# Attention with one score product: probabilities turned on TensorE, and two heads' values on two column halves

## The chip, the core and the metric

The kernel runs on one core of a Trainium2 chip. TensorE (PE) multiplies matrices from SBUF into PSUM; VectorE (DVE), ScalarE (ACT) and GpSimd (POOL) work on rows of both memories; SyncE (SP) and the queues of ACT and POOL issue DMAs. The metric is the device time of one execution in microseconds. The profile is one execution's own record: its *span* goes from the first to the last instruction.

## The reference

One layer of a hybrid encoder takes 1024 tokens of a new stream and 32 tokens of a running one (1056 in all, width 1024). One input projection feeds three mixers: latent attention, an S5 state-space model and an RWKV-7 scan. Their outputs (384, 256 and 384 wide) go through one output projection, a layer norm, and an MLP of squared ReLU. The change is in attention, of 6 heads:

```python
def mla_scores(q_nope, q_rope, k_nope, k_rope):
    s = jnp.einsum('bqhd,bkhd->bhqk', q_nope, k_nope) + jnp.einsum('bqhr,bkr->bhqk', q_rope, k_rope)
    return s.astype(F32) * MLA_SCALE

def attend(s, v, mask=None):
    if mask is not None:
        s = jnp.where(mask, s, NEG_INF)
    p = jax.nn.softmax(s, axis=-1).astype(v.dtype)
    return jnp.einsum('bhqk,bkhd->bqhd', p, v)
```

A head's key has 64 columns of its own and 32 rotary ones shared by the heads; values have 64. Prompt tokens see the 64-token chunks up to their own (the mask); sample tokens see all of 512 cached keys and the 32 new ones.

## The kernel before, in words

The program goes through the input projection, the matrices of the scan, a *middle* part, the output projection with its norm, and the MLP. The middle (from about 246 to 692 us) runs four streams, each a Python generator that yields after a short step: F (`attn_front`), O (`attn_back`), S (the RWKV scan, nine blocks of 128 tokens, the sample's first) and X (S5). `PLAN` is a string with one letter a step. `middle` takes the next letter, makes that stream's step, and lays the step behind the last PE instruction of the step before, so PE's order follows the string closely; two rules turn an F into an O and back when one of them is too far ahead. Within these bounds a scheduler sets the order on the other engines.

Every matrix product that needs near-f32 accuracy and is long is done by `mm3`: each operand is split into a high and a low part of type f32r (`split3`, an ACT copy and a DVE subtraction), and three matmuls (lines 63, 65 and 67) add up. Other products are f32 matmuls, which the profile records as two passes.

Before, a head makes its scores twice. In F, `attn_max` puts tokens on partitions (tile `sc`, one PSUM bank of two, up to 512 keys), masks, and takes each token's maximum on DVE (line 1227). The maxima of nine token tiles are turned on PE (`scm`), split, and sent by four small DMAs into row 96 of the head's query tiles `qh`, `ql`, where the keys hold -1. In O, `attn_out` then puts keys on partitions (tile `st`, up to 512 tokens, 97 rows at work): the maximum is subtracted by the product itself, ACT takes the exponential to `ptk` (line 1281), POOL zeroes the masked quarter (line 1283), and the result is already the moving operand of the value product `av` (line 1256), up to 512 tokens wide. The stationary operand is 128 wide: 64 value columns and 64 columns of ones, so that the sum of the probabilities comes out on the other 64 partitions. Lines 1261 to 1269 copy `av` out (`po`), and multiply by the reciprocal of the sum, made from Ln, Exp and one Newton step, to `ot`. Token blocks are 512, the 32 sample tokens, and 512. Heads 2p and 2p+1 make pair p, which fills 128 rows of `mg_d` in DRAM.

Keys are kept for three heads (`NKT`), queries for two. The queries of all heads are written to DRAM (`q_d`) by `stage_q` and read back by `attn_q`. Behind the middle, `out_early` loads the mixers' outputs of three token tiles into the room of keys and queries, and `out_mm` begins the output projection (`acc<-wo,mh`); the scheduler lays these matmuls among the last attention steps.

In the scan each step uses PE and then DVE or ACT; its PE tiles are named `pra`, `prt`, `prb`, `prk`, `prg`, `pru`, `prn`, `pry`, `prs`, `prm`, `prw`, `prv`, from a ring of three PSUM banks. Most of its matmuls use 64*64 tiles of the array.

Of the kernel before, what the change touches and what calls it, by code (L numbers as in the profile page):

```python
# [8 lines left out]
F32 = mybir.dt.float32  # L9
# [1079 lines left out]
def attn_setup(g):  # L1089

    nc = g.nc
    g.kh, g.kl, g.q2 = [], [], []
# [8 lines left out]
    for x in (kr, g.kpast):  # L1101
        nc.gpsimd.memset(x[96:128], 0.0)
        nc.gpsimd.memset(x[96:97], -1.0)
    for x, o, c, n in ((g.kpast, TP, 0, 512), (kr, 0, 0, TP), (kr, 1536, TP, TS)):
        split3(g, x[64:128, c:c + n], g.kh[0][64:128, o:o + n], g.kl[0][64:128, o:o + n])
    for i in range(NKT):
        for ks in (g.kh, g.kl):
            if i:
                nc.gpsimd.tensor_copy(out=ks[i][64:128], in_=ks[0][64:128])
        for x in g.q2[i] if i < 2 else ():  # L1110
            nc.scalar.activation(out=x[96:128], in_=g.ckv[96:128], func=AF.Copy, scale=0.0)
# [15 lines left out]
def attn_values(g, p):  # L1127

    nc = g.nc
    vo = g.ap.tile([P, 13, 3, 64], F32, tag="vo", name="vo", bufs=1)  # L1130
    nc.gpsimd.memset(vo[:, :, 1], 1.0)
    for q in range(0, 13, 4):
# [6 lines left out]
        nc.scalar.activation(out=vo[:n, q:q + m, 0:3:2], in_=ps[:n, :m].rearrange("p t (h x) -> p t h x", h=2), func=AF.Copy)  # L1139
# [57 lines left out]

def attn_q(g, h):

    nc = g.nc  # L1200
    qh, ql = g.q2[h % 2]
    q = g.ap.tile([P, T], F32, tag="q", name="q", bufs=1)
    nc.sync.dma_start(out=q[0:96], in_=g.q_d[h])
    if h > 1:
        for x in (qh, ql):
            nc.scalar.activation(out=x[96:128], in_=g.kh[0][96:128, 0:T].bitcast(F32), func=AF.Copy, scale=0.0)
# [3 lines left out]
    return qh, ql  # L1210


def attn_max(g, h, qh, ql):

    nc = g.nc
    kh, kl = g.kh[h % NKT], g.kl[h % NKT]
    mx = g.ap.tile([P, 9, 2], F32, tag="mx", name="mx", bufs=2)
    nc.gpsimd.memset(mx, -3.0e38)
    for t in range(9):
        s, n, k0, nk = (t * P, P, 0, (t + 1) * P) if t < 8 else (TP, TS, 1024, 544)  # L1220
        for b in range(0, nk, 512):
            w = min(512, nk - b)
            ps = g.psc.tile([P, 512], F32, tag="sc", name="sc")
            mm3(nc, [ps[:n, :w]], qh[:, s:s + n], ql[:, s:s + n], [(kh[:, k0 + b:k0 + b + w], kl[:, k0 + b:k0 + b + w])], True, True)
            if t < 8 and b + w == nk:
                nc.vector.memset(ps[0:64, w - 64:w], -1e30)
            nc.vector.tensor_reduce(out=mx[:n, t, b // 512:b // 512 + 1], in_=ps[:n, :w], axis=AX.X, op=ALU.max)  # L1227
            yield
    yield
    yield  # L1230
    m9 = g.ap.tile([P, 9], F32, tag="m9", name="m9", bufs=2)
    nc.vector.tensor_tensor(out=m9, in0=mx[:, :, 0], in1=mx[:, :, 1], op=ALU.max)
    ps = g.psc.tile([P, 512], F32, tag="sc", name="scm")
    nc.tensor.transpose(out=ps[0:9, 0:P], in_=m9, identity=g.ident)
    mh = g.ap.tile([9, P], F32R, tag="mh", name="mh", bufs=2)
    ml = g.ap.tile([9, P], F32R, tag="ml", name="ml", bufs=2)
    split3(g, ps[0:9, 0:P], mh, ml)
    for m, q in ((mh, qh), (ml, ql)):
        nc.sync.dma_start(out=q[96:97, 0:TP].bitcast(F32), in_=m[0:8].bitcast(F32))
        nc.sync.dma_start(out=q[96:97, TP:T].bitcast(F32), in_=m[8:9, 0:TS].bitcast(F32))  # L1240


def attn_out(g, h, qh, ql, vo, ot):

    nc = g.nc
    i = h % 2
    kh, kl = g.kh[h % NKT], g.kl[h % NKT]
    rows, srow = hsl(i), hsl(1 - i)
    late = None

    def av(s, n, kt, c, w, pt, tiles, po=[None]):

        if kt == tiles[0]:
            po[0] = g.pav.tile([P, 512], F32, tag="av", name="av")
        po = po[0]
        nc.tensor.matmul(out=po[:, c:n], lhsT=vo[:w, kt].rearrange("p a x -> p (a x)")[:, 64 * i:64 * i + P], rhs=pt[:w, c:n],  # L1256
                         start=kt == tiles[0], stop=kt == tiles[-1])
        if kt < tiles[-1]:
            return
        x = g.ap.tile([P, 512], F32, tag="ptk", name="po", bufs=g.npt)  # L1260
        nc.scalar.activation(out=x[:, :n], in_=po[:, :n], func=AF.Copy)  # L1261
        rec = g.ap.tile([P, 512], F32, tag="rec", name="rec", bufs=1)
        rt = g.ap.tile([P, 512], F32, tag="rt", name="rt", bufs=1)
        nc.scalar.activation(out=rec[srow, :n], in_=x[srow, :n], func=AF.Ln)
        nc.scalar.activation(out=rec[rows, :n], in_=rec[srow, :n], func=AF.Exp, scale=-1.0)
        nc.vector.tensor_copy(out=rt[rows, :n], in_=x[srow, :n])
        nc.vector.tensor_tensor(out=rt[rows, :n], in0=rt[rows, :n], in1=rec[rows, :n], op=ALU.mult)
        nc.vector.scalar_tensor_tensor(out=rec[rows, :n], in0=rt[rows, :n], scalar=2.0, in1=rec[rows, :n], op0=ALU.subtract, op1=ALU.mult)
        nc.vector.scalar_tensor_tensor(out=ot[rows, s:s + n], in0=x[rows, :n], scalar=-1.0, in1=rec[rows, :n], op0=ALU.mult, op1=ALU.mult)
        if i == 1:  # L1270
            store(g, nc.sync if h == 5 and s == 512 else None, g.mg_d[h // 2, :, s:s + n], ot[:, s:s + n])

    for s, n in ((0, 512), (TP, TS), (512, 512)):
        tiles = range((s + n) // P) if n > TS else range(8, 13)
        for kt in tiles:
            c = max(0, kt * P - s) if n > TS else 0
            w = P if kt < 12 else TS
            ps = g.pst.tile([P, 512], F32, tag="st", name="st")
            mm3(nc, [ps[:w, c:n]], kh[:, kt * P:kt * P + w], kl[:, kt * P:kt * P + w], [(qh[:, s + c:s + n], ql[:, s + c:s + n])], True, True)
            pt = g.ap.tile([P, 512], F32, tag="ptk", name="ptk", bufs=g.npt)  # L1280
            nc.scalar.activation(out=pt[:w, c:n], in_=ps[:w, c:n], func=AF.Exp, scale=MLA_SCALE)
            if n > TS and kt * P >= s:
                nc.gpsimd.memset(pt[64:128, c:c + 64], 0.0)
# [4 lines left out]
            late = s, n, kt, c, w, pt, tiles  # L1288
    av(*late)


NKT = 3
# [7 lines left out]
def attn_front(g):  # L1300
# [4 lines left out]
    for h in range(6):  # L1305
        if h % 2 == 0:
            yield from attn_keys(g, h // 2)
# [1088 lines left out]
```

## Time and profile before

| what | value |
|---|---|
| median of 3 runs (lowest, highest) | 1469.61 us (1469.31, 1478.45) |
| profiled execution | 1466.29 us |
| its span | 1464.5 us |
| granted PE clock, mean | 0.976 |

In a row of a stretch stands the busy time of each engine, with its number of instructions. In a row of the timeline stand start and duration of one or several equal instructions; on PE the durations of neighbours overlap. "128*64" is the part of the array that a matmul uses, rows by columns, and "128x512" what one instruction works on. A wait is put down to whatever released the waiting instruction last.

### The profile page before, as it was taken

What the parts mean: (1) busy time and instruction counts of PE and PEld (TensorE: products, weight loads), DVE (VectorE), ACT (ScalarE), POOL (GpSimd) and SP (SyncE); (2) the same over time, 40 slices, a digit from 0 to 9 for tenths busy, and PEclk for the clock granted to TensorE, in tenths of its full rate; (3) what the DMA queues carried; (4) which work ended last, traced back from release to release, by engine and by line L of the source; (5) the groups of instructions that cost most, each with busy time, mean ns of one, the idle gap of its engine ahead of it and who ended that gap; (6) DMA issues with size and microseconds to landing.
All of it is one profiled execution on the core that took longest, in us unless ns stands there. A gap on an engine that the chain in (4) does not pass through costs nothing.

```text
span 1464.5 us, 28210 instructions
## 1 busy us (share of the span) xinstructions
PE 1376.6 (94%) x11527; PEld 1237.8 (85%) x11527; DVE 986.2 (67%) x1752; ACT 643.6 (44%) x1126; POOL 186.5 (13%) x285
## 2 busy tenths in 40 slices
PE   7999999698999879889899899999999999999996
PEld 6989898476777657667589899999999999999995
DVE  8767979654656635653858976666656686665577
ACT  5544645334554554542426444444444443334332
POOL 2412110401111111220530000000000000000023
PEclk9999999899999989989999999999999999999998
DMA  5315464671343320241634344443329795354222
GB/s 201 146 67 189 143 183 101 150 154 50 91 106 87 87 54 28 70 122 44 201 119 138 129 182 136 162 143 145 142 89 386 256 307 176 91 178 131 62 102 76
DMA packets 150326, 198.59 MB, mean 136 GB/s; under 512 B 53392, under 2 KB 98116, under 8 KB 149688
## 3 DMA queue, kind: packets, MB, share of 16 engines
q1 hardware_dynamic: 129396, 175.91, 37.4%
q10 hardware_dynamic: 20448, 19.88, 4.4%
q8 instruction: 90, 1.47, 0.4%
q0 software_dynamic: 352, 1.01, 0.2%
q14 instruction: 40, 0.33, 0.1%
HBM read 129.42 MB, written 67.28 MB: 134 GB/s over the span
## 4 chain that ended last, share of the span: by engine, by line
PE 79%; DVE 8%; DMA 5%; ACT 3%; issue 2%; SPq 1%; ACTq 0%; POOL 0%; DVEq 0%; POOLq 0%
PE acc L63 20%; PE acc L65 20%; PE acc L67 19%; PE av L1256 3%; PE st L65 1%; PE st L63 1%; PE st L67 1%; DVE mx L1227 1%; PE prw L883 1%; PE sc L63 1%; PE scv L1138 1%; DMA xr<-in_xt 1%; DMA mraw<-mg_d 1%; PE prt L841 1%; DMA wr<-in_w_up 1%
## 5 line engine op out<-in xcount | busy, mean ns | idle before, releaser
L63 PE MATMUL acc<-xo,wo 128*128 128x272 f32 (+1 forms) x896 | 254.8, 285 | 2.8 <-ACT wo L49 2.8
L67 PE MATMUL acc<-xo,wo 128*128 128x256 f32 (+1 forms) x896 | 253.9, 285 | 1.9 <-DVE wo L50 1.9
L65 PE MATMUL acc<-xo,wo 128*128 128x272 f32 (+1 forms) x896 | 253.7, 284 | 0.0
L67 PE MATMUL acc<-hop,wo 128*128 128x272 f32 (+1 forms) x896 | 193.9, 283 | 0.0
L63 PEld LDWEIGHTS acc<-xo,wo 128*128 128x128 f32 x896 | 168.8, 189 | 3.0 <-ACT wo L49 3.0
L67 PEld LDWEIGHTS acc<-xo,wo 128*128 128x128 f32 x896 | 168.8, 189 | 2.3 <-DVE wo L50 2.3
L65 PEld LDWEIGHTS acc<-xo,wo 128*128 128x128 f32 x896 | 169.1, 189 | 0.0
L65 PE MATMUL acc<-hop,wo 128*128 128x272 f32 (+1 forms) x768 | 158.6, 284 | 0.0
L63 PE MATMUL acc<-hop,wo 128*128 128x256 f32 (+1 forms) x768 | 158.3, 284 | 0.0
L67 PEld LDWEIGHTS acc<-hop,wo 128*128 128x128 f32 x896 | 142.7, 188 | 0.0
L63 PE MATMUL acc<-xh,wmhi 128*128 128x384 f32 (+3 forms) x384 | 127.6, 333 | 7.8 <-ACT xh L49 7.8
L65 PE MATMUL acc<-xl,wmhi 128*128 128x384 f32 (+3 forms) x384 | 128.3, 334 | 2.5 <-DVE xl L50 2.5
L67 PE MATMUL acc<-xh,wmlo 128*128 128x384 f32 (+3 forms) x384 | 126.1, 328 | 0.0
L65 PEld LDWEIGHTS acc<-hop,wo 128*128 128x128 f32 x768 | 119.2, 188 | 0.0
L63 PEld LDWEIGHTS acc<-hop,wo 128*128 128x128 f32 x768 | 118.1, 188 | 0.0
L2134 POOL TENSOR_TENSOR wr<-wr,gb 128x512 f32<-128x512 f32 (+1 forms) x14 | 19.8, 1437 | 672.6 <-ACT wr L2132 672.6
L49 ACT ACTIVATE wo<-wr 128x512 fp32r<-128x512 f32 (+1 forms) x64 | 47.0, 739 | 117.1 <-PE acc L67 70.1
L1256 PE MATMUL av<-ptk,vo 128*128 128x512 f32 (+5 forms) x204 | 74.9, 453 | 14.0 <-ACT po L1261 9.3
L63 PEld LDWEIGHTS acc<-xh,wmhi 128*128 128x128 f32 (+1 forms) x384 | 71.3, 186 | 10.6 <-ACT xh L49 8.3
L50 DVE TENSOR_TENSOR hop<-hraw,hop 128x1056 fp32r<-128x1056 f32 (+3 forms) x58 | 70.4, 1213 | 14.3 <-ACT hop L49 14.2
L50 DVE TENSOR_TENSOR wo<-wr,wo 128x512 fp32r<-128x512 f32 (+1 forms) x64 | 52.3, 820 | 39.4 <-ACT wo L49 39.4
L65 PEld LDWEIGHTS acc<-xl,wmhi 128*128 128x128 f32 (+1 forms) x384 | 71.4, 186 | 7.2 <-DVE xl L50 3.9
(543 smaller groups left out, 3086.6 us busy)
## 6 DMA issues: line engine op xcount, KB each, us to landing
hraw<-h_d SPq DMA_DIRECT2D x48, 528.0 KB, 3.6
wr<-in_w_up SPq DMA_DIRECT2D x35, 512.0 KB, 3.9
h_d<-hx SPq DMA_DIRECT2D x16, 792.0 KB, 3.3
h_d<-ht SPq DMA_DIRECT2D x16, 792.0 KB, 4.6
wd<-in_w_dn SPq DMA_DIRECT2D x16, 512.0 KB, 6.2
wr<-in_w_dn SPq DMA_DIRECT2D x16, 512.0 KB, 5.0
ld<-rw SPq DMA_DIRECT2D x24, 320.0 KB, 4.5
wmraw<-in_w_m SPq DMA_DIRECT2D x12, 512.0 KB, 4.5
```

The source lines that it names most:

```text
L49: nc.scalar.activation(out=hi, in_=ps, func=AF.Copy)
L50: (lo_eng or nc.vector).tensor_tensor(out=lo, in0=ps, in1=hi.bitcast(F32), op=ALU.subtract)
L63: nc.tensor.matmul(out=outs[i], lhsT=lh, rhs=rhs[i][0], start=start, stop=False, **kw)
L65: nc.tensor.matmul(out=outs[i], lhsT=lh, rhs=rhs[i][1], start=False, stop=False, **kw)
L67: nc.tensor.matmul(out=outs[i], lhsT=ll, rhs=rhs[i][0], start=False, stop=stop, **kw)
L841: nc.tensor.transpose(out=pt[:, i], in_=ld[:, p, i], identity=g.ident)
L883: nc.tensor.matmul(out=pw[hsl(c), p - p0, h], lhsT=g.xt[p][hsl(c), t, h], rhs=r[hsl(c), p, K_A:K_NV + 1:K_NV, h], start=True, stop=True)
L1138: nc.tensor.matmul(out=ps[:n, j], lhsT=c, rhs=g.wkv[:, 1, p * P:p * P + P], start=True, stop=True)
L1227: nc.vector.tensor_reduce(out=mx[:n, t, b // 512:b // 512 + 1], in_=ps[:n, :w], axis=AX.X, op=ALU.max)
L1256: nc.tensor.matmul(out=po[:, c:n], lhsT=vo[:w, kt].rearrange("p a x -> p (a x)")[:, 64 * i:64 * i + P], rhs=pt[:w, c:n], start=kt == tiles ...
L2134: nc.gpsimd.tensor_tensor(out=o[:n, c], in0=o[:n, c], in1=g.gb2[:n, 0, c], op=ALU.mult)
```

## The change

Scores are made once, with tokens on partitions, and the exponential is taken there. `attn_rows` (stream F) goes through groups of one token tile, for both heads of a pair: product and masked maximum per part of up to 512 keys as before, then the smaller of the two negated maxima times the scale (DVE), then the exponential straight from the score banks with that as bias, which also adds up the row (`accum_out`). A score bank is so held until its exponential is done. The probabilities of a group and head stay in SBUF (`p`, six buffers).

`attn_out` (stream O) then turns each key tile's probabilities on PE, for two heads into one bank (`pt`), copies them out by DVE or ACT in turn (`ptk`, two buffers), and multiplies: each head has 64 value columns as stationary operand, on its own column half of the array, so that the two heads' outputs fill the 128 partitions of one bank. Masked keys are already zero, as the exponential of a masked score. The reciprocal of each token's sum is made on a column of 128 tokens, spread over 64 columns (`nb`), and turned on PE into the same bank (columns from 256 on); one DVE operation multiplies at the end. Ones in the values, POOL's zeroes, row 96 and its DMAs go. The shared key rows are copied between the two key buffers by two DMAs of ACT's queue and no longer by POOL. The query loads are issued one head ahead.

`PLAN` is another string, 557 letters and not 527; S and X have as many as before (132, 38).

```diff
-    kr = g.ap.tile([P, 13 * 3 * 64], F32, tag="vo", name="kr", bufs=1)[:, :T]
+    kr = g.ap.tile([P, T], F32, tag="q", name="kr", bufs=NQB)
...
-                nc.gpsimd.tensor_copy(out=ks[i][64:128], in_=ks[0][64:128])
+            nc.scalar.dma_start(out=ks[i][64:96].bitcast(F32), in_=ks[0][64:96].bitcast(F32))
...
+GROUPS = ((0,), (1,), (2,), (3,), (8,), (4,), (5,), (6,), (7,))
+def attn_rows(g, p, j):
+    sm = g.ap.tile([P, 2, 2, 2], F32, tag="sm", name="sm", bufs=2)
+    for i in range(2):
+        (qh, ql), kt = g.q2[i], (2 * p + i) % NKT
+        kh, kl = g.kh[kt], g.kl[kt]
+        for r, t in enumerate(GROUPS[j]):
+            s, n, k0, nk = (t * P, P, 0, (t + 1) * P) if t < 8 else (TP, TS, 1024, 544)
+            x = g.ap.tile([P, 1024], F32, tag="p", name="p", bufs=NPB)
...
+            for c, b in enumerate(range(0, nk, 512)):
+                if c:
+                    yield
+                w = min(512, nk - b)
+                ps = g.psc.tile([P, 512], F32, tag="sc", name="sc")
+                mm3(nc, [ps[:n, :w]], qh[0:96, s:s + n], ql[0:96, s:s + n], [(kh[0:96, k0 + b:k0 + b + w], kl[0:96, k0 + b:k0 + b + w])], True, True)
+                if t < 8 and b + w == nk:
+                    nc.vector.memset(ps[0:64, w - 64:w], -1e30)
+                nc.vector.tensor_reduce(out=mx[:n, c:c + 1], in_=ps[:n, :w], axis=AX.X, op=ALU.max, negate=True)
+                parts.append((ps[:n, :w], b, w))
...
+            for c, (ps, b, w) in enumerate(parts):
+                nc.scalar.activation(out=x[:n, b:b + w], in_=ps, func=AF.Exp, scale=MLA_SCALE, bias=mx[:n, 2:3], accum_out=sm[:n, i, r, c:c + 1])
+            xs[i, r] = x
+            yield
...
+def attn_out(g, p, j, vo, ot):
...
+    S.activation(out=y, in_=a, func=AF.Ln)
+    S.activation(out=y, in_=y, func=AF.Exp, scale=-1.0)
+    V.tensor_tensor(out=t, in0=a, in1=y, op=ALU.mult)
...
+        V.scalar_tensor_tensor(out=nb[:n, r], in0=bc(t[:, :, r:r + 1], [n, 2, 64]), scalar=2.0, in1=bc(y[:, :, r:r + 1], [n, 2, 64]), op0=ALU.subtract, op1=ALU.mult)
+    po = g.pav.tile([P, 512], F32, tag="av", name="av")
+    for r in range(m):
+        nc.tensor.matmul(out=po[:, 256 + n * r:256 + n * r + n], lhsT=nb[:n, r].rearrange("p i x -> p (i x)"), rhs=g.ident[:n, :n], start=True, stop=True)
+    S.activation(out=rb, in_=po[:, 256:256 + n * m], func=AF.Copy)
+    def av(k, w, c, halves, first, last):
+        for i in range(2):
+            nc.tensor.matmul(out=po[hsl(i), c:n * m], lhsT=vo[:w, k, 64 * i:64 * i + 64], rhs=halves[i], start=first, stop=last, tile_position=(0, 64 * i))
...
+        for k in range(last + 1):
...
+                    nc.tensor.transpose(out=ps[:, i, (r - r0) * P:(r - r0) * P + P], in_=xs[i, r][:, k * P:k * P + P], identity=g.ident)
...
+            if k % 2:
+                S.activation(out=e, in_=ps, func=AF.Copy)
+            else:
+                V.tensor_copy(out=e, in_=ps)
+            yield
+            if late:
+                av(*late)
+                yield
+            late = k, P, r0 * P, [e[:, i] for i in range(2)], k == 0, k == last
+        av(*late)
+    V.scalar_tensor_tensor(out=ot[:, s:s + n * m], in0=po[:, 0:n * m], scalar=-1.0, in1=rb, op0=ALU.mult, op1=ALU.mult)
...
-NKT = 3
+NKT = 2
+NPB = 6
+NPT = 2
+NQB = 1
...
-            if c == "F" and fronts > backs + 1:
+            if c == "F" and g.probs >= NPB:
                 c = "O"
...
-    "FFFFFFFFFFFSFFFFFFSFFFFFFSFFFFSFFFFSOOOSOFSOOOSFOOSOOOOSFSSOSFOOOOFSOOSXFOOOSFOOSXOOOOFFOOOSFSSSOSSO"
+    "FFFFFFFFSFFFFFFFFSFSOSFFSFSFOSOSSOOSOFSOFSOFOSOOSOFSOSXXFOSOFOSFOSFOSOFSOFSOFOSXOFSOFSOSFOXSSOSFOFOF"
```

What this moves on PE shows at two places. First, in the scan's stretch, between the state products (`pry`, `prs`) of a block and its `prw`. Before:

```order
L941 MATMUL pry<-gq,st 64x64 x6
L945 MATMUL prs<-st,gq 64x64 x6
L63 MATMUL sc<-kh,qh 128x256
L65 MATMUL sc<-kl,qh 128x256
L67 MATMUL sc<-kh,ql 128x256
L969 MATMUL prm<-yb,bones 128x384
L883 MATMUL prw<-r,xt 64x128 x12
L1256 MATMUL av<-ptk,vo 128x512
L63 MATMUL st<-qh,kh 128x512
L65 MATMUL st<-ql,kh 128x512
L67 MATMUL st<-qh,kl 128x512
```

Now, at the same place of a block:

```order
L1275 MATMUL av<-ptk,vo 64x128 x2
L941 MATMUL pry<-gq,st 64x64 x6
L945 MATMUL prs<-st,gq 64x64 x6
L1300 MATMUL pt<-ident,p 128x128 x2
L63 MATMUL sc<-kh,qh 128x512
L65 MATMUL sc<-kl,qh 128x512
L67 MATMUL sc<-kh,ql 128x512
L969 MATMUL prm<-yb,bones 128x384
L883 MATMUL prw<-r,xt 64x128 x12
```

The second score product (`st`) and the wide `av` are gone; a pair of turns (`pt`) or of 64-column `av` stands beside a scan step, and one score triple between F steps as before.

Second, behind the scan's last matmul (`prv`). Before:

```order
L986 MATMUL prv<-sq,bones 128x384
L1256 MATMUL av<-ptk,vo 128x512
L63 MATMUL st<-qh,kh 128x512
L65 MATMUL st<-ql,kh 128x512
L67 MATMUL st<-qh,kl 128x512
```

Now, some rows behind `prv`:

```order
L1130 MATMUL scv<-wkv,ckv 128x128 x4
L1130 MATMUL scv<-wkv,cpast 128x128 x4
L1130 MATMUL scv<-wkv,ckv 32x128
L1269 MATMUL av<-ident,nb 128x128
L1300 MATMUL pt<-ident,p 128x128 x2
L1275 MATMUL av<-ptk,vo 64x128 x2
L63 MATMUL sc<-kh,qh 128x512
L65 MATMUL sc<-kl,qh 128x512
L67 MATMUL sc<-kh,ql 128x512
```

Before, only the last head's second half stood there; now pair 2 begins there, with its values (`scv`) and its first token tiles, and the rest of its scores, turns and value products follow behind the scan's end, with no scan step among them.

More of the change, by code (lines that the diff above doesn't have):

```diff
@@ L1099, in attn_setup @@
             g.q2.append([g.ap.tile([P, T], F32R, tag=f"q{x}{i}", name="q" + x, bufs=1) for x in "hl"])
-    for x in (kr, g.kpast):
-        nc.gpsimd.memset(x[96:128], 0.0)
-        nc.gpsimd.memset(x[96:97], -1.0)
     for x, o, c, n in ((g.kpast, TP, 0, 512), (kr, 0, 0, TP), (kr, 1536, TP, TS)):
-        split3(g, x[64:128, c:c + n], g.kh[0][64:128, o:o + n], g.kl[0][64:128, o:o + n])
-    for i in range(NKT):
+        split3(g, x[64:96, c:c + n], g.kh[0][64:96, o:o + n], g.kl[0][64:96, o:o + n])
+    for i in range(1, NKT):
         for ks in (g.kh, g.kl):
-            if i:
-                nc.gpsimd.tensor_copy(out=ks[i][64:128], in_=ks[0][64:128])
-        for x in g.q2[i] if i < 2 else ():
-            nc.scalar.activation(out=x[96:128], in_=g.ckv[96:128], func=AF.Copy, scale=0.0)
+            nc.scalar.dma_start(out=ks[i][64:96].bitcast(F32), in_=ks[0][64:96].bitcast(F32))
 def attn_keys(g, p):
@@ L1129, in attn_values @@
     nc = g.nc
[L1130 to L1131 removed]
+    vo = g.ap.tile([P, 13, P], F32, tag="vo", name="vo", bufs=1)
     for q in range(0, 13, 4):
@@ L1138, in attn_values @@
             nc.tensor.matmul(out=ps[:n, j], lhsT=c, rhs=g.wkv[:, 1, p * P:p * P + P], start=True, stop=True)
-        nc.scalar.activation(out=vo[:n, q:q + m, 0:3:2], in_=ps[:n, :m].rearrange("p t (h x) -> p t h x", h=2), func=AF.Copy)
+        n = P if q < 12 else TS
+        nc.scalar.activation(out=vo[:n, q:q + m], in_=ps[:n, :m], func=AF.Copy)
         yield
@@ L1195, in stage_q, with attn_load @@
         nc.gpsimd.dma_start(out=g.q_d[4 + h, 64:96], in_=qb[32 * h:32 * h + 32])
+def attn_load(g, h):
+    g.qr[h] = g.ap.tile([P, T], F32, tag="q", name="q", bufs=NQB)
+    g.nc.sync.dma_start(out=g.qr[h][0:96], in_=g.q_d[h])
 def attn_q(g, h):
-    nc = g.nc
     qh, ql = g.q2[h % 2]
[L1202 to L1206, printed above, removed]
+    q = g.qr.pop(h)
     for s, n in ((0, 512), (512, 544)):
@@ L1209, in attn_q @@
         yield
-    return qh, ql
-def attn_max(g, h, qh, ql):
+GROUPS = ((0,), (1,), (2,), (3,), (8,), (4,), (5,), (6,), (7,))
+GM = max(map(len, GROUPS))
+def attn_rows(g, p, j):
     nc = g.nc
[L1216 to L1227, printed above, removed]
-            yield
[L1229 to L1240, printed above, removed]
@@ L1243, in attn_out @@
-def attn_out(g, h, qh, ql, vo, ot):
-    nc = g.nc
[L1246 to L1283, printed above, removed]
@@ L1287, in attn_out @@
                 yield
-            late = s, n, kt, c, w, pt, tiles
-    av(*late)
-NKT = 3
+            late = k, P, r0 * P, [e[:, i] for i in range(2)], k == 0, k == last
+        av(*late)
+    V.scalar_tensor_tensor(out=ot[:, s:s + n * m], in0=po[:, 0:n * m], scalar=-1.0, in1=rb, op0=ALU.mult, op1=ALU.mult)
+    g.probs -= 2 * m
+    store(g, nc.sync if p == 2 and j == len(GROUPS) - 1 else None, g.mg_d[p, :, s:s + n * m], ot[:, s:s + n * m])
+NKT = 2
+NPB = 6
+NPT = 2
+NQB = 1
 def last_traced(g, engine):
@@ L1304, in attn_front @@
     attn_setup(g)
-    for h in range(6):
-        if h % 2 == 0:
-            yield from attn_keys(g, h // 2)
-        g.qs[h] = yield from attn_q(g, h)
-        yield from attn_max(g, h, *g.qs[h])
-        yield h
-def attn_back(g):
-    for h in range(6):
-        if h % 2 == 0:
-            g.vo = yield from attn_values(g, h // 2)
-            g.ot = g.ap.tile([P, T], F32, tag="ot", name="ot", bufs=1)
-        yield from attn_out(g, h, *g.qs.pop(h), g.vo, g.ot)
-        yield h
+    g.qr = {}
+    for h in range(NQB):
+        attn_load(g, h)
+    for p in range(3):
+        yield from attn_keys(g, p)
+        for i in range(2):
+            h = 2 * p + i
+            yield from attn_q(g, h)
+            if h + NQB < 6:
+                attn_load(g, h + NQB)
+        for j in range(len(GROUPS)):
+            yield from attn_rows(g, p, j)
+            yield j
+def attn_back(g):
+    for p in range(3):
+        vo = yield from attn_values(g, p)
+        ot = g.ap.tile([P, T], F32, tag="ot", name="ot", bufs=1)
+        for j in range(len(GROUPS)):
+            yield from attn_out(g, p, j, vo, ot)
+            yield j
 def middle(g, scan):
-    g.npt, g.qs, g.late = 5, {}, []
+    g.late, g.probs = [], 0
     streams = {"F": attn_front(g), "O": attn_back(g), "S": scan, "X": stage_s5(g)}
```

59 lines of the change are left out of this document (52 added, 7 removed).

## The prediction

> **What bounds the kernel now.** I read the page's head first, then the busy time by stretches, the waits of TensorE (PE) in the attention stretch, and last the times at which single PE instructions start. The columns of the stretches are PE, its weight loads, DVE, ACT and POOL busy, the granted clock, the DMA share and the rate.
>
> ```profile
> PE 1376.6 (94%) x11527; PEld 1237.8 (85%) x11527; DVE 986.2 (67%) x1752; ACT 643.6 (44%) x1126; POOL 186.5 (13%) x285
> ```
>
> ```profile
> 246.00:308.00 62.00, 48.12 (x510) 34.72 (x510) 42.41 (x76) 23.44 (x47) 18.12 (x20) 0.86 0.66 151
> 308.00:667.00 359.00, 321.67 (x3488) 242.08 (x3482) 204.49 (x447) 180.80 (x373) 55.47 (x115) 0.95 0.30 81
> 667.00:689.00 22.00, 22.00 (x92) 16.37 (x91) 3.09 (x7) 4.22 (x10) 3.42 (x7) 1.00 0.05 14
> ```
>
> The program is held by PE nearly throughout. Only 246 to 689 us is touched: in the middle row attention (streams F and O), the RWKV scan (S) and S5 (X) share PE, which is busy 90% of it, DVE 57%, ACT 50%. So PE work taken out counts there, unless waits take its place. The waits that PE has in 246 to 692 (total, times, longest):
>
> ```profile
> PE sc L63 <- DVE mx L1227: 11.7, 11, 2.9
> ...
> PE av L1256 <- ACT po L1261: 9.3, 2, 8.7
> PE av L1256 <- POOL ptk L1283: 4.7, 5, 2.4
> PE st L63 <- DMA qh<-mh: 2.4, 1, 2.4
> ...
> PE st L65 <- DMA ql<-ml: 1.5, 2, 1.0
> ```
>
> **PE work removed.** A matmul's own duration holds pipeline time that overlaps the next, so I price by distances of starts. How many there are:
>
> ```profile
> L63 PE MATMUL st<-qh,kh x102: 178/442/818, 308.7 to 682.8; 128*128 128x512 f32 x36, 128*128 128x32 f32 x24, 128*128 128x384 f32 x12, 128*128 128x256 f32 x12
> ```
>
> ```profile
> L1256 PE MATMUL av<-ptk,vo x204: 190/483/1222, 310.6 to 688.6; 128*128 128x512 f32 x36, 128*128 128x32 f32 x24, 128*128 128x384 f32 x12, 128*128 128x256 f32 x12
> ```
>
> The four commonest shapes are named; by the loop the rest of the 102 are 12 of 128 columns and 6 of 32 with 32 keys. Each score stands in three such groups (lines 63, 65, 67); an av matmul is recorded as two passes. The unit prices:
>
> ```profile
> 432.70 0.39 PE L65 MATMUL st<-ql,kh 128*128 128x512 f32 x1
> 432.93 0.39 PE L67 MATMUL st<-qh,kl 128*128 128x512 f32 x1
> 433.16 0.22 PE L63 MATMUL sc<-kh,qh 128*128 128x128 f32 x1
> ```
>
> ```profile
> 502.22 0.26 PE L65 MATMUL st<-ql,kh 128*128 128x32 f32 x1
> 502.33 0.26 PE L67 MATMUL st<-qh,kl 128*128 128x32 f32 x1
> 502.44 0.39 PE L1256 MATMUL av<-ptk,vo 128*128 128x32 f32 x2
> 502.66 0.26 PE L63 MATMUL st<-qh,kh 128*128 128x32 f32 x1
> ```
>
> ```profile
> 668.51 0.86 PE av L1256 x2
> ...
> 682.58 0.65 PE av L1256 x2
> ```
>
> A 512-column score pass takes 0.23 us, so 384 and 256 columns some 0.175 and 0.12; 32 columns take 0.11, a floor that I also give to 128. An f32 av takes 0.86 at 512, 0.65 at 384 (the last two rows, from the chain), so 0.43 and 0.22 at 256 and 128, and 0.22 at 32. The Trainium skill (TensorE: Matmul & The Clock Gate, LDWEIGHTS) gives a weight load its columns divided by 1.2 in ns; by it 128 columns take 107 ns, and the floor of 0.11 agrees.
>
> Scores with keys on partitions: 36 x 3 x 0.23 + 12 x 3 x (0.175 + 0.12 + 0.11) + 24 x 3 x 0.11 = 24.8 + 14.6 + 7.9 = 47.3 us (the 18 smallest at nothing). The av: 36 x 0.86 + 12 x (0.65 + 0.43 + 0.22) + 30 x 0.22 = 31.0 + 15.6 + 6.6 = 53.2. Removed: 100.5.
>
> **PE work added.** Per pair there are 36 key tiles of the prompt and 5 of the sample, in each a transpose for each head and one *set*: two 64-column f32 matmuls, so four passes.
>
> ```profile
> 719.10 1.31 PE pt L1522 x12
> ```
>
> ```profile
> 434.30 1.46 PE prw L883 x24
> ```
>
> Transposes like the 12 here (0.109 each): 216 x 0.109 + 30 x 0.11 = 26.8. The sums' reciprocals, 27 f32 matmuls at 0.22: 6.0. A 128-column pass alone costs about 0.11, yet prw's 24 passes on 64*64 tiles last 1.46, that is 13 slots and not 24: a tile's second pass runs beside the next tile's first. Four passes on two column tiles are then 3 slots, 0.33: 123 sets are 40.6; serial they would be 54.1. I take the overlap, as prw is the nearest row. The Trainium skill's figure would put a 64-column load at 53 ns, an estimate by which the 15 sample sets could be about half as dear. Added: 73.4; net **-27.1**, or -13.6 without overlap.
>
> Does going in and out of column tiles cost? Two neighbours, one of 64-row tiles and one with 64 columns:
>
> ```profile
> 443.34 0.58 PE L847 MATMUL prb<-ld 64*64 64x64 f32 x24
> 443.85 0.50 PE L63 MATMUL sc<-kh,qh 128*128 128x512 f32 x1
> 444.18 0.39 PE L65 MATMUL sc<-kl,qh 128*128 128x512 f32 x1
> ```
>
> ```profile
> 663.02 0.49 PE L954 MATMUL prq<-ident,st 128*64 128x128 f32 x3
> 663.34 0.81 PE L969 MATMUL prm<-yb,bones 128*128 128x384 f32 x2
> ```
>
> The 24 prb passes, four tiles at 0.053, should take 0.32; 0.51 pass, and the next score needs 0.33 for 0.23: 0.3 us for an excursion. The three prq at 128*64 take 0.32, their bare work, and nothing follows. The Trainium skill (TensorEngine Tiling (Array Packing), Key Properties) says that a change of tiling mode drains TensorE; prb agrees, prq shows no such drain. I take 0 as the nearer shape and keep 0.3 a set for a rival.
>
> **Waits that go.** The waits for po, the masked ptk and the maxima's DMAs vanish with their causes: 9.3 + 4.7 + 2.4 + 1.5 = 17.9, **-18**. The wait for the maximum stays and gets dearer, since a score bank is now held until the exponential has read it, for a row of two parts until both maxima are there.
>
> ```profile
> L1227 DVE TENSOR_REDUCE mx<-sc 128x1 f32<-128x512 f32 x36 | 24.6, 687 | 17.5 <-PE sc L67 17.0
> ```
>
> ```profile
> L1281 ACT ACTIVATE ptk<-st 128x512 f32<-128x512 f32 x36 | 21.5, 596 | 30.4 <-PE st L67 30.1
> ...
> L1281 ACT ACTIVATE ptk<-st 128x256 f32<-128x256 f32 x12 | 4.6, 381 | 17.6 <-PE st L67 17.4
> ```
>
> Such a row takes two score triples (2 x 0.7), the last maximum 0.69 and one exponential 0.60 before its first bank is free, with drains and small steps about 3.2 us, of which PE works 1.4. There are 10 such rows a pair. While the scan runs, S and O stand between F steps (the order's first place), which leaves I estimate 0.5 us for each of 20: **+10**. After the scan's last step stands nearly all of pair 2 (the second place), with F and O alone: 10 rows at about 1 us, and 36 key tiles whose multiply waits on a copy (0.38 plus drain, against one transpose pair of 0.22 ahead of it) at about 0.3: **+21**, bounds 0 and 40.
>
> **Moved or hidden.** The exponentials pass from 102 to 84 instructions over the same scores. Copies of the turned probabilities (108 x about 0.38, halved between ACT and DVE) take the room of the old normalization on 64x512; both engines stay far below PE's share. Score matmuls keep their price on 96 rows, as columns set it. The key rows' copy goes from POOL to two DMAs of 196 KB on ACT's queue, ahead of head 1's first scores; I cost it at nothing behind the first queries' trip through DRAM, else one landing of this kind, 4.5 us:
>
> ```profile
> ld<-rw SPq DMA_DIRECT2D x24, 320.0 KB, 4.5
> ```
>
> The stage's end gets shorter:
>
> ```profile
> 688.96 0.61 ACT po L1261
> ...
> 692.36 0.70 DVE ot L1269
> ```
>
> From 688.96 to 693.06 six operations of 0.6 to 0.7 follow each other before the last store; now there is one DVE operation: **-3**.
>
> **Sum.** -27 - 18 + 10 + 21 - 3 = -17 us. The profiled execution took 1466.3 (span 1464.5 and 1.8 around it), 3.3 below the median of 1469.6. So 1449 in that execution's terms, 1452.6 as a median: I say **1452**. With bounds (13 for the overlap, 20 on either side after the scan, 10 for the scan's row waits) the forecast's own range is 1428 to 1474.
>
> **Rivals.** *The scan sets the pace (slower).* Pair 2 leaves the scan's stretch: 24 of the added 73 us and some 16 of scores, priced like a third of st, where about 9 of attention stood behind the scan before. So the sum needs that stretch to shrink from 359 us by 31, by 20 of the net work and 18 of waits, less 10: to 300, or 33.3 for each of the scan's nine blocks, where 39.9 pass now. Its quickest block in the trace, from prn to prn:
>
> ```profile
> 426.42 0.91 PE L869 MATMUL prn<-r 64*64 64x64 f32 x24
> ```
>
> ```profile
> 459.71 0.51 PE L869 MATMUL prn<-r 64*64 64x64 f32 x10
> ```
>
> That is 33.3 too, with PE full of attention, so it was not the scan that held it back; for the rival: no block was quicker, and scan steps that follow each other wait for DVE and ACT. Each us a block is 9 us: no gain from 35.3, over 1% slower from 36.9. At 38 it would be 1452 + 9 x 4.7 = 1494. Chance 0.20, half of it within 1%.
>
> *Column tiles drain like 64-row tiles (slower or no change).* 123 sets x 0.3 = +37: 1489; from 0.14 us a set the gain is gone. Prb speaks for, prq against. 0.13.
>
> *The gain goes into the part after the scan.* F and O alone, two score banks, one output bank: at the upper bound of 40 and no gain from the waits, 1452 + 19 + 10 = 1481, no change that counts. 0.17.
>
> *More goes than I count.* With the row waits hidden (-10) and half of those after the scan (-10): 1432; 0.15. The forecast itself has 0.35.
>
> **How the numbers follow.** About 1% (14.7 us, so below 1455 or above 1484) is what this kernel's measurements tell from no change. Faster: 0.15 + 0.25 of the forecast + 0.08 of the others' milder ends = 0.48. Slower: 0.10 of the scan + 0.07 of the tiles + 0.02 = 0.19. Same: 0.33. The range, 1428 to 1492, holds the forecast, the quicker case and the rivals' milder halves.
>
> **What would show it.** Right: groups st gone, pt about 24 us by starts, a set in 0.33 to 0.35 us, the last prv near 608 us instead of 666, the last av near 680. Wrong: starts after a set late by 0.2 or more (tiles); the scan's prn rows still 36 us or more apart (scan); over 95 us between the last prv and the out projection's dense part, or PE waits for p, ptk or mx above 45 us (after the scan).

## The result, and the profile after

The changed kernel takes 1510.7 us (median of 4 runs, 1505.4 to 1517.9), the kernel before 1469.5: a ratio of 1.027, with a 95% interval of 1.022 to 1.033. It is slower by 41 us; forecast was a gain of 17. The profiled execution took 1505.4 us, with a span of 1503.6; it is the quickest of the four and has the highest granted clock (0.948, the others 0.939 to 0.941), so the rows below show less half clock than the median run has.

First the page's busy times and the clock in 40 slices of the span, then the stretches from the scan's first step to its last, from there to attention's last multiply, and on through the output projection to the MLP's first matmul (columns as in the prediction).

```profile
PE 1391.7 (93%) x11803; PEld 1241.7 (83%) x11803; DVE 995.8 (66%) x1881; ACT 648.9 (43%) x1252; POOL 160.2 (11%) x220
...
PEclk9999999689999889758999999999999999999998
```

```profile
310.00:620.00 310.00, 266.77 (x3371) 196.15 (x3371) 187.74 (x472) 157.88 (x393) 39.44 (x60) 0.91 0.35 88
620.00:733.00 113.00, 92.98 (x481) 65.44 (x479) 37.92 (x115) 35.10 (x108) 10.55 (x9) 0.79 0.06 17
733.00:821.00 88.00, 83.04 (x388) 63.39 (x386) 59.01 (x88) 27.27 (x75) 33.22 (x28) 0.98 0.44 143
```

The same stretch of the kernel before, cut at its own first and last scan step (its 22 us behind the scan stand in the prediction):

```profile
310.00:667.00 357.00, 319.67 (x3435) 240.40 (x3435) 202.60 (x443) 180.47 (x373) 55.47 (x115) 0.95 0.30 81
```

The middle went from 357 + 22 = 379 us to 310 + 113 = 423. The scan's stretch is shorter by 47, the part behind it longer by 91, and there the clock was 0.79. In each stretch I call *dead* the time in which PE is idle, and the time lost to the clock, which is the length times what the clock lacks to 1. Idle moments inside a stretch of half clock are counted in both, so it is a rough measure.

| stretch | length | idle | lost to the clock |
|---|---|---|---|
| before, scan | 357 | 37 | 18 |
| before, behind it | 22 | 0 | 0 |
| after, scan | 310 | 43 | 28 |
| after, behind it | 113 | 20 | 24 |

Dead time rose from 55 to 115 us. What is left, PE's work, fell from 324 to 308, so by 16, where the forecast had 27. So, by this measure, both halves of the sum failed: less work went than counted, and far more dead time came. The clock's part can be checked on whole executions, as each one records its mean clock: the span times what that clock lacks to 1 is 88 us for the changed kernel (mean of its four) and 37 to 39 for the kernel before (four sets of 8 to 25 executions, run beside the experiments).

PE's waits from 246 to 760 us (total, times, longest), and below them a piece of its timeline behind the scan (start, duration, line, operation; in brackets the idle time ahead of it and what ended it):

```profile
PE sc L63 <- ACT p L1240: 27.1, 15, 3.9
...
PE pry L941 <- DVE st L948: 5.2, 3, 2.8
```

```profile
644.75 0.79 PE L63 MATMUL sc<-kh,qh 96*128 96x512 f32 x1 [1.31 <-ACT p L1240]
645.34 0.63 PE L65 MATMUL sc<-kl,qh 96*128 96x512 f32 x1
645.77 0.63 PE L67 MATMUL sc<-kh,ql 96*128 96x512 f32 x1
646.20 0.31 PE L63 MATMUL sc<-kh,qh 96*128 96x128 f32 x1
646.30 0.41 PE L65 MATMUL sc<-kl,qh 96*128 96x128 f32 x1
646.51 0.41 PE L67 MATMUL sc<-kh,ql 96*128 96x128 f32 x1
648.74 0.79 PE L63 MATMUL sc<-kh,qh 96*128 96x512 f32 x1 [1.81 <-ACT p L1240]
649.34 0.63 PE L65 MATMUL sc<-kl,qh 96*128 96x512 f32 x1
```

Line 1240 is the exponential that empties a score bank. Two things are to be seen. The next head's first score waits 1.81 us for it. And the 512-column passes around the gap follow each other in 0.43 to 0.60 us, where the prediction's rows have 0.23: PE runs at half its clock here. Whether the gaps bring the half clock is asked by runs 1, 4 and 9.

Where the clock is full, the steps of one key tile look like this:

```profile
455.19 0.38 PE L1300 MATMUL pt<-ident,p 128*128 128x128 f32 x2
455.40 0.62 PE L632 MATMUL s5e<-ut,em 128*128 128x133 f32 x4
```

```profile
432.03 0.44 PE L1275 MATMUL av<-ptk,vo 128*64 128x128 f32 x4
432.40 0.33 PE L63 MATMUL sc<-kh,qh 96*128 96x128 f32 x1
432.56 0.27 PE L65 MATMUL sc<-kl,qh 96*128 96x128 f32 x1
...
433.98 0.44 PE L1300 MATMUL pt<-ident,p 128*128 128x128 f32 x2
434.34 0.44 PE L1275 MATMUL av<-ptk,vo 128*64 128x128 f32 x4
434.71 0.33 PE L907 MATMUL pru<-wu,r 64*64 64x64 f32 x2
```

Two turns ahead of work on the whole array hold PE for 0.21 us (455.19 to 455.40), ahead of a set for 0.36 (433.98 to 434.34). The set itself takes 0.37, and a 128-column pass behind it 0.16 instead of the forecast's 0.11. So a set in column tiles costs 0.15 + 0.37 + 0.05 = 0.57 us by these rows, 0.24 more than forecast. Most of it stands ahead of the set and in it; a pass behind a whole-array group can be late as well (run 7).

### The profile page after: what moved, and what is told of

It is laid out like the page before. It is cut to its first block, busy times and chain, and to the rows that moved or that the text cites. A ratio compares the mean times of both kernels' runs of the same rounds, so it can differ in the third digit from the quotient of the medians.

```text
span 1503.6 us, 28940 instructions
## 1 busy us (share of the span) xinstructions
PE 1391.7 (93%) x11803; PEld 1241.7 (83%) x11803; DVE 995.8 (66%) x1881; ACT 648.9 (43%) x1252; POOL 160.2 (11%) x220
## 4 chain that ended last, share of the span: by engine, by line
PE 62%; DVE 7%; ACT 4%; DMA 3%; issue 2%; SPq 1%; POOL 0%; ACTq 0%; DVEq 0%; POOLq 0%
PE acc L63 16%; PE acc L65 16%; PE acc L67 16%; PE av L1275 2%; PE pt L1300 2%; PE sc L63 1%; DMA wo<-in_w_out 1%; ACT p L1240 1%; PE sc L67 1%; PE sc L65 1%; PE s5g L693 1%; DVE wo L50 1%; DVE mx L1233 1%; DMA em<-em_d 1%; DMA mraw<-mg_d 1%
## 5 line engine op out<-in xcount | busy, mean ns | idle before, releaser
L63 PEld LDWEIGHTS acc<-xh,wmhi 128*128 128x128 f32 (+1 forms) x384 | 72.3, 188 | 10.9 <-ACT xh L49 8.2
L63 PE MATMUL sc<-kh,qh 96*128 96x512 f32 (+4 forms) x84 | 40.7, 485 | 39.9 <-ACT p L1240 27.1
```

What stands on the lines that cost most here:

```text
L63: nc.tensor.matmul(out=outs[i], lhsT=lh, rhs=rhs[i][0], start=start, stop=False, **kw)
```

## The experiments

**The theories.** *Held banks*: PE waits for score banks that wait for their exponentials, and the gaps bring the half clock. *The way in and out of the column tiles* (the drain, in the expectations) costs 0.2 us. *Order*: what stands behind the scan's last step stands wrongly. *Packing* (the first rival of the forecast): the scan, at 33 us a block, sets the pace. No kernel here leaves work out; some add products that nobody reads. Ratios are to the kernel before, with 95% intervals. A gain over the changed kernel is uncertain by some 8 to 10 us either way, as that kernel has four runs.

**1. More banks.** In the last pair, from its third row on, every other score part goes into the ring of the scan, which is nearly idle by then.

```diff
+                spare = p == 2 and j > 1 and (i + c) % 2
-                ps = g.psc.tile([P, 512], F32, tag="sc", name="sc")
+                ps = (g.pr if spare else g.psc).tile([P, 512], F32, tag="pr" if spare else "sc", name="sc")
```

> Half of pair 2's score parts (from the third token tile on) take a bank of the scan's ring, which is idle by then, so that a part needs not wait for the exponential of the part before the last. If held score banks make the 113 us behind the scan (620 to 733 us), PE's waits for the exponential there fall from some 30 us to under 10, the half clock goes with them, that stretch comes to about 80 us and the time to about 1475. If the stretch is held by something else (ACT's queue, the copies of turned tiles, or column tiles), it stays within 5 us of 113.

1484.6 us, ratio 1.011 (1.007 to 1.014): 26 us quicker than the changed kernel. Its stretches, cut likewise, and its wait for the exponential:

```profile
307.00:622.00 315.00, 273.86 (x3373) 201.95 (x3373) 187.81 (x472) 158.19 (x393) 39.42 (x60) 0.88 0.33 87
622.00:709.00 87.00, 77.38 (x482) 56.12 (x482) 37.37 (x114) 32.64 (x108) 10.46 (x9) 0.97 0.08 22
```

```profile
PE sc L63 <- ACT p L1241: 13.3, 6, 3.9
```

Behind the scan, 113 us became 87: idle time fell from 20 to 10, the clock's loss from 24 to 3. That the held banks cost this is shown, and the half clock there went along with them. In the scan's stretch, where hardly anything changed, the clock was 0.88 and not 0.91: one execution differs from another by some 10 us there.

**2. Both heads on the whole array.** Instead of two products on column halves, one product of 128 value columns with both heads' probabilities, 256 columns wide; the half that isn't wanted is computed too.

```diff
-        for i in range(2):
-            nc.tensor.matmul(out=po[hsl(i), c:n * m], lhsT=vo[:w, k, 64 * i:64 * i + 64], rhs=halves[i], start=first, stop=last, tile_position=(0, 64 * i))
+        nc.tensor.matmul(out=po[:, 0:2 * n].rearrange("p (i t) -> p i t", i=2), lhsT=vo[:w, k], rhs=halves, start=first, stop=last)
```

> Both heads' values as one 128-wide stationary operand on the whole array, against both heads' probabilities as one moving operand of 256 columns; the two useful quarters of the result are taken at the end by two DVE operations. No column tiles any more, but no overlap of passes: two passes of 256 columns, 0.43 us, where a set of four overlapping passes should take 0.33. If going in and out of column tiles is free, 123 sets cost 0.1 more each: +12 us. If it costs what the turns and sets beside each other show (0.37 + 0.37 us for a pair of turns and a set, where 0.22 + 0.33 were counted), about -10 us; if it costs 0.3, -25.

1515.3 us, ratio 1.033 (1.028 to 1.037), whose interval overlaps that of the changed kernel. The column halves bring nothing measurable over the plain form. But the gain of 10 to 25 us that a price for the way in and out should have given did not come either, and why isn't settled: the edit also takes a second DVE operation per row group.

**3. Order alone.** The scan's and S5's letters are spaced evenly, up to nine tenths of attention's.

> The same steps, but from the 61st letter of the string on the scan's and S5's letters stand evenly among the attention's, up to nine tenths of these, so that pair 2's rows have scan steps between them. If it is the order that costs (attention alone behind the scan), PE's waits for the exponential fall below 20 us in all and the time falls by 20 to 35 us. If held banks cost as much anywhere, the waits only move into the scan's stretch and the time stays within 8 us of 1510.

1517.9 us, ratio 1.035 (1.031 to 1.038).

```profile
305.00:697.00 392.00, 317.51 (x3637) 231.23 (x3633) 214.39 (x564) 183.14 (x478) 43.18 (x62) 0.86 0.28 73
697.00:740.00 43.00, 42.63 (x218) 30.45 (x218) 11.20 (x24) 8.40 (x22) 7.44 (x7) 0.93 0.05 13
```

The part behind the scan is short and dense, and nothing is won: the scan's stretch has 74 us of idle time, and waits for the exponential there are 32.4 us (11.4 up to 625 us in the changed kernel). Work that isn't planned around the waits carries them along. This order differs from the old one everywhere, so the run doesn't say what the best order would give.

**4. The clock alone.** In the last five row groups, four unread 512-column products stand behind each head's scores, so that PE is busy in the gap.

> Four matmuls of 512 columns whose result nobody reads, behind each head's scores of pair 2's last five rows: 0.9 us of PE work at full clock into gaps of 1.8 us. Adds work, leaves none out. If the half clock behind the scan is a cost of its own beside the waits, it goes for most of the stretch and the time falls by 8 to 15 us in spite of the added work. If the chain of maximum and exponential sets the pace there whatever the clock, the time stays within 3 us.

1517.8 us, ratio 1.035 (1.031 to 1.039).

```profile
621.00:743.00 122.00, 107.38 (x526) 75.72 (x525) 37.60 (x115) 34.52 (x108) 10.52 (x9) 0.78 0.05 16
695.00:705.00 10.00, 10.00 (x41) 6.15 (x41) 2.58 (x7) 2.03 (x6) 0.67 (x1) 0.51 0.09 29
```

Idle time fell from 20 to 15, the clock stayed at 0.78, and the filler cost 7 us: neither expectation came. The second row speaks against the gaps as what holds the clock down: for 10 us PE has no idle time at all, and the clock is 0.51. More than half of that stretch are turns and sets, one after the other; whether these count less for the clock than other matmuls was not tested. The filler itself stands in the order ahead of work that could have run.

**5. Half the ways in and out.** Two key tiles are turned in two steps, then both sets are made in one.

```diff
-            if late:
-                av(*late)
+            if k:
+                if k % 2 and k > 1:
+                    av(*late.pop(0))
+                    av(*late.pop(0))
                 yield
```

> The changed kernel, with the sets of two key tiles put next to each other: two steps turn two key tiles, the next step makes both sets, so 51 or so of the 123 excursions into the column tiles serve two sets and some 57 excursions go; the work and the table of steps stay. If an excursion costs 0.2 us of drain on its two sides (rows of the changed kernel), 57 x 0.2 = 11 us go: 1499, against 1511. If the drain is nothing (the forecast's value) 1511, give or take 4 for the shifted steps. If instead the dense sets need their multiply apart from the copies, it gets worse in the part after the scan: a tail above 118 us, 1515 or more.

1498.7 us, ratio 1.019 (1.017 to 1.021): 12 us quicker. An excursion is a run of sets with nothing between them on PE. The changed kernel's trace has 103 (the sample's five sets share one, and some sets meet), this run's has 52, so 51 went and not 57 as expected. 12 us by 51 are 0.24 us for one, with an interval of some 0.1 to 0.4. Its timeline:

```profile
697.04 0.66 PE L1300 MATMUL pt<-ident,p 128*128 128x128 f32 x4
697.63 0.66 PE L1275 MATMUL av<-pts,vo 128*64 128x128 f32 x8
698.12 0.61 PE L1275 MATMUL av<-ptk,vo 128*64 128x128 f32 x8
698.65 0.50 PE L63 MATMUL sc<-kh,qh 96*128 96x512 f32 x1
```

Eight passes behind eight others take 0.49 us (697.63 to 698.12), so a set inside a run of sets is 0.25: below the forecast's 0.33. The overlap was there; alone between other work a set loses it.

**6 and 7. The price by itself.** The kernel before, with two unread f32 products of 128 columns in front of each of the 102 score triples st: once on the two column halves, once on the whole array.

```diff
+            for z in range(2):
+                nc.tensor.matmul(out=ps[hsl(z), 0:P], lhsT=g.ckv[:, 64 * z:64 * z + 64], rhs=g.ckv[:, 0:P], start=True, stop=True, tile_position=(0, 64 * z))
```

> The kernel before, with two unread f32 multiplies of 64 columns by 128, on the two column halves, in front of each of the 102 score triples st, into the bank that the scores then overwrite. No bank is held longer and no wait is added, so it prices the excursion alone. Passes that overlap as forecast: 102 x 0.33 = 34 us. Theory of a drain of 0.2 us an excursion: 34 + 20 = 54, so 1523. Theory of no drain: 1503, and 11 us quicker than the same with whole-array multiplies.

> The twin of the run before: the same two unread multiplies, but on the whole array, 128 columns by 128, so four passes of 0.11 each and no change of tiles: 102 x 0.44 = 45 us, 1514 under both theories. What counts is its distance to the run with column halves: 9 us quicker than that by the drain, 11 us slower without it.

1511.0 us (1.0277, 1.0253 to 1.0300) on the halves, 1502.9 (1.0222, 1.0198 to 1.0247) on the whole array: the halves are 8 us dearer, with an interval of about 3 to 13, and not 11 cheaper. The 1523 that the drain gave for the halves alone was too high. First the halves, then the whole array:

```profile
714.82 1.02 PE L1256 MATMUL av<-ptk,vo 128*128 128x512 f32 x2
715.77 0.44 PE L1280 MATMUL st<-ckv 128*64 128x128 f32 x4
716.14 0.50 PE L63 MATMUL st<-qh,kh 128*128 128x512 f32 x1
716.48 0.40 PE L65 MATMUL st<-ql,kh 128*128 128x512 f32 x1
```

```profile
699.57 1.02 PE L1256 MATMUL av<-ptk,vo 128*128 128x512 f32 x2
700.43 0.61 PE L1280 MATMUL st<-ckv 128*128 128x128 f32 x4
700.79 0.48 PE L63 MATMUL st<-qh,kh 128*128 128x512 f32 x1
701.11 0.39 PE L65 MATMUL st<-ql,kh 128*128 128x512 f32 x1
```

On the halves, the av ahead takes 0.95 for 0.86, the four passes 0.37, the next pass 0.34 for 0.23: 0.57 together. On the whole array the av takes its 0.86, the passes 0.36, the next 0.32 for 0.23: 0.45. By these rows the difference would be 12 us for 102. Both runs added less than the rows give (41 for 58, 33 for 46). PE's idle time fell by some 4 us in each, so a part of the added work went into waits that were there; where the rest went is open.

**8. Banks and pairs.** Edits 1 and 5 together.

> The changed kernel with both: the scan's idle banks for half of the last pair's score parts (26 us in the earlier run), and the sets of two key tiles next to each other (11 us by the theory of the drain). If the two causes are separate they add up: 1511 - 26 - 11 = 1474. If the drain is nothing, 1485 as with the banks alone. If the paired sets only fill waits that the banks have already taken away, 1480 to 1485.

1481.2 us, ratio 1.007 (1.004 to 1.009). 30 us are gained and not 38. The missing 8 lie within the uncertainty of the three gains, so the run doesn't tell whether the two causes are separate.

**9. Evenly mixed behind the scan.** Behind the scan's last step, the same F and O letters in even order, where runs of five F stood (the last two lines of the table).

> The changed kernel with the letters behind the scan's last step put in another order: the same score steps (F) and output steps (O), but evenly mixed, where runs of five F stood between runs of O. The banks are held as long as before; now output work stands behind a score part while its bank waits. Theory of the held banks: the gap of 1.9 us in each two-part row shrinks to some 0.8, PE's idle time behind the scan from 20 to about 8 us and with it the half clock there from 47 to about 15 (16 us at half speed): 1511 - 12 - 16 = 1483. If the gaps come from the exponentials' engine as such, or from the copies of the turned probabilities, mixing changes nothing: 1505 to 1515.

1498.0 us, ratio 1.021 (1.017 to 1.025): 13 quicker, half of what was expected.

```profile
615.00:718.00 103.00, 93.05 (x485) 65.03 (x483) 36.95 (x115) 34.86 (x108) 10.46 (x9) 0.79 0.07 19
```

```profile
641.00:678.00 37.00, 32.71 (x131) 21.53 (x131) 13.42 (x42) 13.76 (x44) 2.72 (x2) 0.50 0.09 25
```

The idle time went from 20 to 10 as expected, and the clock stayed at 0.79. In one stretch of 37 us PE is busy 88% of the time and yet at half clock throughout. As in run 4, the idle time that the profile shows doesn't tell the half clock.

**10. Early exponential.** The first part of a two-part row goes through its exponential from its own maximum at once. With the second maximum, the stored half and its sum are scaled to the row's maximum.

```diff
+                nc.scalar.activation(out=x[:n, b:b + w], in_=ps[:n, :w], func=AF.Exp, scale=MLA_SCALE, bias=mx[:n, 2 + c:3 + c], accum_out=sm[:n, i, r, c:c + 1])
...
+                nc.scalar.activation(out=f[:n], in_=mx[:n, 1:2], func=AF.Exp)
+                nc.vector.tensor_scalar(out=x[:n, 0:512], in0=x[:n, 0:512], scalar1=f[:n], scalar2=None, op0=ALU.mult)
```

> The changed kernel, in which the first part of a two-part row goes through its exponential at once, from its own maximum; when the second maximum is there, the stored first half and its sum are multiplied by exp(own maximum - row maximum), which is four small operations and one of 512 columns on DVE more for each of 30 rows. The first bank is free after one reduction and one exponential (1.4 us) and no more after both parts (3.2). Theory of the held banks: half of the 27 us of waits for p goes, in the scan's stretch and behind it, and about as much half clock: some -15, so 1495. If the time of hold is not the cause: 1511, or more by the added DVE work.

1491.7 us, ratio 1.018 (1.014 to 1.021): 19 quicker, though DVE has more to do. Its waits, and the stretch behind the scan:

```profile
PE sc L63 <- ACT p L1238: 10.9, 13, 1.7
```

```profile
614.00:715.00 101.00, 89.10 (x483) 63.08 (x484) 44.51 (x154) 35.14 (x117) 10.79 (x9) 0.85 0.07 19
```

The wait for the exponential fell from 27.1 to 10.9 us, and its longest from 3.9 to 1.7: it was the first part's wait for the second that held the bank.

**11 and 12. All together.** Edits 1, 5 and 9, and then 10 as well.

> The changed kernel with three edits: idle scan banks for the last pair's parts, paired sets, evenly mixed letters behind the scan. The first two together gave 1481, with 5 us of idle time and 13 of half clock left behind the scan (12 us in all). If the mixing takes most of that: 1471 to 1474. If the banks have already taken all that order can give: 1481.

> The three edits and the early exponential. What is left to win stands in the scan's stretch: 49 us of idle time and 61 of half clock where the kernel before had 37 and 37 (24 us dearer in all), and of that the waits for the exponential are some 13. If the early release takes these: 1471 - 8 to 10 = 1462. If the waits there are of other kinds: 1471 or what the run without it gives.

1475.2 us (1.004, 1.002 to 1.006) and 1466.3 us (0.9993, 0.9975 to 1.0011): with all four the kernel is level with the one before. The last one's stretches, and its largest waits within the scan's:

```profile
306.00:612.00 306.00, 260.55 (x3375) 197.97 (x3374) 203.37 (x555) 161.94 (x413) 40.26 (x60) 0.89 0.34 90
612.00:691.00 79.00, 74.97 (x482) 58.06 (x480) 44.21 (x153) 34.16 (x117) 10.70 (x9) 0.93 0.08 25
```

```profile
PE pry L941 <- DVE st L948: 6.1, 4, 3.1
PE prq L954 <- DVE st L948: 5.8, 2, 3.6
PE pry L941 <- ACT yb L920: 5.0, 2, 2.6
...
PE sc L63 <- ACT p L1239: 2.9, 3, 1.5
```

Behind the scan little is dead now. In the scan's stretch there are still 45 us of idle time and 34 lost to the clock, and attention's wait for the exponential is only 2.9 of it: 26 are the scan's own steps (pry, prq, prs and others), waiting for DVE and ACT, and the rest is spread over S5 and attention's copies.

**13 to 15. A looser table.** Edits as in 12, and each S and X stands behind 1.1, 1.2 or 1.3 times as many letters of attention.

> The changed kernel with the four edits so far (scan banks, paired sets, even letters behind the scan, early exponential; 1466), and the scan's letters stretched: each S and X stands behind 1.1 times as many F and O letters, so that the scan ends at 0.76 of these letters where it ended at 0.70, and some 16 us of attention move from behind the scan into it. The scan's stretch holds 45 us of idle time and 65 of half clock, now mostly waits between scan steps for DVE and ACT. If the scan, packed into 33 us a block, is what is left (the forecast's first rival): the moved work fills its gaps and the time falls by 6 to 16, to 1450 to 1460. If the gaps come from attention's own waits they come along: 1466 or more.

> As before, but stretched by 1.2: the scan ends at 0.82 of the letters, some 36 us of attention move into it. Scan theory: 1440 to 1455. Theory that order can't win more: 1466 or more, as attention alone already runs with 4 us of idle time behind the scan.

> As before, stretched by 1.3: the scan ends at 0.88 of the letters. Scan theory: as 1.2 or a few us more, since some gaps remain whatever fills them. Other theory: above 1470, since scan steps that each wait for DVE and ACT then lie in line with more of attention's waits, as in the run with the letters spread evenly.

1481.0 (1.006, 1.003 to 1.008), 1470.5 (1.000, 0.998 to 1.002) and 1464.9 us (0.996, 0.994 to 0.998). Neither theory has this order, with the least stretch the slowest: there the wait for the exponential is back at 14.3 us. The last is the only kernel here that beats the one before, by 0.4%. Its stretches and waits within the scan's:

```profile
309.00:646.00 337.00, 288.47 (x3599) 223.97 (x3596) 229.04 (x663) 181.87 (x496) 37.86 (x60) 0.91 0.32 82
646.00:689.00 43.00, 42.83 (x248) 32.06 (x246) 18.89 (x43) 11.85 (x36) 10.64 (x9) 0.97 0.12 36
```

```profile
PE pry L941 <- DVE st L948: 8.5, 4, 4.4
PE prv L986 <- ACT sq L973: 4.8, 1, 4.8
```

36 us moved from behind the scan into it, and it grew by 31: the idle time there stayed, 48 us where it was 45. That speaks against the packing as such, as a looser scan should have fewer waits; but the three tables also move every letter against every other. Which letter would have to stand at which scan step was not tried.

## Why the prediction was wrong

**PE work removed, turns, end of the stage.** The st groups are gone, two turns take 0.21 (0.22 forecast), and from the last multiply to the MLP it is 88 us where it was 91: the -3 was right.

**The sets.** "I take 0 as the nearer shape" is the first step that failed. A set alone between other work costs 0.57 and not 0.33. 103 ways in and out at 0.24 (run 5) are 25 us, more than the 14 that the overlap of the halves was to save. The rival of the column tiles had the mechanism, at 0.3 for each of 123 sets. Run 2, whose gain should have shown the same price, doesn't bear it out, so the size is less sure than the sign. The three prq that spoke against it do show no such cost; they are transposes that all lie on the same column half, and why they differ stays open. The Trainium skill (TensorEngine Tiling (Array Packing), Key Properties) says that a change of tiling mode drains TensorE; runs 5 to 7 agree with it for these shapes, at about 0.2 us for the way in and out (0.24 by run 5).

**Waits that go, waits that come.** The waits for po, the masked ptk and the maxima's DMAs went as said. For those of the held banks the forecast had 10 in the scan and 21 behind it; PE's waits for p are 11.4 up to 625 us and 15.8 behind the scan. So the size of this term was right. Two steps failed beside it. First, the forecast priced all work at the full clock: behind the scan it fell to 0.79, which cost another 24 us, and in the scan it took 10 more than before. The bound of 40 for the part behind the scan was too low: idle time and clock are 44, and 32 of the 103 ways in and out lie there too. With the banks freed (run 1) that half clock went along with the gaps; runs 4 and 9 kept it with fewer of them, so what brings it is open. Second, the sum has nothing for the scan's own steps (pry, prs, pru, prq, prv): they wait 17 us for DVE and ACT up to 625 us, where they waited 4 in the whole of the stretch before.

**The scan's stretch.** Forecast were 300 us, and the last prv near 608; it was 310 and 620. The blocks came as forecast: from prn to prn it is 33.1 us on the mean (319.4 for the first, 584.2 for the last), so the sign of the first rival, 36 or more, did not come. What is off is the division by nine. The stretch has eight such distances, and 9 us ahead of the first prn and 36 behind the last one; the 39.9 us of a block before were 37.8 from prn to prn. By the rival's price the 10 us would leave a gain, and runs 13 to 15 speak against its mechanism too: the stretch keeps 48 to 51 us of idle time at every looser density tried. Open is how much of it a better place for single steps would remove.

**The rivals.** The third, that the gain goes into the part behind the scan, came nearest by its mechanism, though its upper bound gives 1481. Of its two signs one came: 113 us from the last prv to the last multiply, behind which the output projection runs alone, where 95 were the bound. The other, PE waits for p above 45 us, did not (27.1), as much of the cost stands in the clock and in no wait.

**The sum of it.** The sets (25 us), the clock (34 in the two stretches) and the scan's own waits (13) overlap in part and make up the miss of 58 us; they can't be added. 1511 less the four edits is 1466, where 1452 was forecast. By the rough measure above, run 12 has 89 us of dead time in 385 and so 296 of work, 28 less than before, about the 27 of the forecast. Dead time is 34 more than before, 24 of it in the scan's stretch, and takes it back.

## What to carry to other kernels

Price a group on a part of the array from the start of what stands ahead of it to the end of its effect on what follows, not by its own length, and put groups of the same shape next to each other. When a score bank is held until a whole row is done, count the time from its first product to its release; the cheap mends are a second ring that is idle then, or a consumer that needs only its own part. When work moves to where its stream runs alone, price it at the clock that such a stretch gets, and read that clock from a trace: PE's busy share doesn't tell it here. Count a chain's blocks from step to like step, and its head and tail apart.

## What the runs showed that was not expected

- PE stands at half its clock for long with gaps of no more than 1.3 to 1.9 us, and also with none (run 4: 10 us at 0.51). Behind the scan of the changed kernel, 20 us ran at 0.50 with PE busy two thirds of the time:

```profile
657.00:677.00 20.00, 13.43 (x61) 10.08 (x63) 7.16 (x22) 6.01 (x24) 0.00 (x0) 0.50 0.01 2
692.00:733.00 41.00, 40.47 (x231) 27.94 (x230) 7.44 (x18) 7.30 (x21) 3.97 (x4) 1.00 0.04 12
```

  Later, with the last scores through and the output projection's matmuls among the attention steps (the second row), the clock is full. The Trainium skill (TensorE: Matmul & The Clock Gate, HAM oscillation — how this bites in real kernels) tells of such falls for waits that outlast the gate's window of 3.4 us, and in the section behind it (A second HAM failure mode: psum-queue depth-cycling) for small idle times between groups; no wait for a bank here lasts 2 us behind the scan, so the rows above fit the second. The rows of runs 4 and 9, at half clock with PE busy all of 10 us and 88% of 37 us, fit neither: what the gate counts as busy is not settled here.
- Four f32 passes on two column halves take 0.25 us in a run of them, but 0.57 alone between work on the whole array, where the whole array takes 0.45 for the same number of passes (run 7).
